# The down projection of a feed-forward layer: seven block products in place of eight, with the weight sums on VectorE and one of them made by a transfer

## The chip, the cores and the metric

The kernel runs on one core of a Trainium2 chip. The metric is device microseconds from start to end of one execution, lower is better; the time before is a median over three runs. One further execution was recorded by the hardware profiler, and every row below is from that one. The engines are TensorE (PE, its weight loads PEld), VectorE (DVE), ScalarE (ACT), GpSimd (POOL) and SyncE (SP, which here only issues transfers).

## The reference

Two layers run one after the other on 512 tokens of width 2048. The change touches only the end of the second:

```python
        x = x + y @ w_out[l]
        h = rms_norm(x, norm2_g[l])
        x = x + (jax.nn.silu(h @ ffn_w_gate[l]) * (h @ ffn_w_up[l])) @ ffn_w_down[l]
    return rms_norm(x, final_norm_g)
```

The hidden width is 5632, which the kernel cuts into 11 chunks of 512. `ffn_w_down` is 5632 x 2048, in float32.

## The kernel before

Every float32 matrix product is made of three matmuls: `split` (L135) turns a tile into a high half (`h`, an ACT cast, L136) and the rest (`l`, a DVE subtraction, L122), and the products high x high, low x high and high x low are summed in PSUM. For weights these halves are called `wh` and `wl`, for the other operand `op`. All float32 DVE additions and subtractions stand in the profile under L122, all matmuls under L112, transposes under L116.

`finish` makes the feed-forward layer in two stages. In the **gate and up stage** `fast_group` (L1632) computes, for each of the 11 chunks, both projections at once by seven products of half-size blocks in place of eight; the weight sums are formed by DVE in the raw tiles `fr` before they are split. The chunk's hidden state is transposed on PE, copied to a tile `v` by ACT (L1785) and written to the DRAM buffer `ud` (`ud<-v`).

In the **down stage** `facc` (512 tokens x 2048, float32 in SBUF) is first loaded with the residual `x3d` (L1794). `hidden(c)` (L1798) loads one chunk of `ud`, 1 MB, and splits it. `down(c)` (L1805) goes over four column blocks of 512: `block` loads the weights two 128-row blocks at a time (512 KB, `raw`), splits them (`wh`, `wl`, 128x1024), and issues 4 x 4 x 3 matmuls into four PSUM banks `psm`; DVE adds each bank to `facc` (128x512). Ten chunks make 10 x 4 x 48 = 1920 matmuls of 128x512. The **last chunk** has its weights and operand split ahead (matmuls `psm<-op,op`, 192 of them) and goes by token tile, since squares, the norm and the output transfers follow each.

No order is written out by hand: a scheduler places each engine's instructions by the program's order and by priorities (`tc.high_priority(self.ahead)` lets weight loads and splits stand far ahead of their matmuls). Each engine and each DMA queue takes its instructions strictly in that order. Pools with a fixed number of buffers decide when a tile may be written again, and memory of a closed pool is used again by the pools that open next.

## Time and the profile before

| | |
|---|---|
| median of 3 runs | 3528.2 us (3525.5 to 3532.1) |
| profiled execution | 3527.2 us |
| its span, first to last instruction | 3525.1 us |
| mean granted TensorE clock | 0.985 |
| PE busy | 3439.2 us, 98% |
| DVE busy | 2205.1 us, 63% |

Busy shares are means over the whole span, in which the gate and up stage takes some 870 us, the down stage 447 us and the last chunk with the end 58 us. Starts in the rows are us from the span's start. "Idle before" is the time for which an engine stood still ahead of an instruction, with the releaser behind it. A granted clock of 1.00 is full speed, 0.50 half of it.

### The profile page before, as it was taken

What the parts mean: (1) busy time and instruction counts of PE and PEld (TensorE: products, weight loads), DVE (VectorE), ACT (ScalarE), POOL (GpSimd) and SP (SyncE); (2) the same over time, 40 slices, a digit from 0 to 9 for tenths busy, and PEclk for the clock granted to TensorE, in tenths of its full rate; (3) what the DMA queues carried; (4) which work ended last, traced back from release to release, by engine and by line L of the source; (5) the groups of instructions that cost most, each with busy time, mean ns of one, the idle gap of its engine ahead of it and who ended that gap; (6) DMA issues with size and microseconds to landing.
All of it is one profiled execution on the core that took longest, in us unless ns stands there. A gap on an engine that the chain in (4) does not pass through costs nothing.

```text
span 3525.1 us, 48425 instructions
## 1 busy us (share of the span) xinstructions
PE 3439.2 (98%) x18730; PEld 2740.2 (78%) x18730; DVE 2205.1 (63%) x3480; ACT 1368.6 (39%) x2239; POOL 53.7 (2%) x50
## 2 busy tenths in 40 slices
PE   7999999999999999999999998999999999999998
PEld 3488887777778787788777787888888888788887
DVE  4367875566555455764566547778878778555545
ACT  3234444555433323432233334444444445322212
POOL 0000000000000000000000000000000000000000
PEclk8999999999999999999999999999999999999999
DMA  8823333222343443434434543443333334533333
GB/s 283 282 85 93 111 114 107 72 81 60 92 145 124 138 131 97 117 109 135 129 107 142 159 142 119 132 125 120 108 114 119 120 120 155 185 120 120 101 96 107
DMA packets 352601, 442.21 MB, mean 125 GB/s; under 512 B 45871, under 2 KB 200179, under 8 KB 351731
## 3 DMA queue, kind: packets, MB, share of 16 engines
q1 hardware_dynamic: 349456, 437.82, 40.7%
q8 instruction: 147, 2.41, 0.3%
q10 hardware_dynamic: 2915, 1.29, 0.1%
q14 instruction: 83, 0.68, 0.1%
HBM read 383.45 MB, written 55.57 MB: 125 GB/s over the span
## 4 chain that ended last, share of the span: by engine, by line
PE 90%; DMA 5%; DVE 3%; ACT 1%; issue 1%; SPq 0%; DVEq 0%; POOL 0%; POOLq 0%; ACTq 0%
PE acc L112 40%; PE pp L112 24%; PE psm L112 23%; DMA wm<-in_w_mod_dram 3%; PE psm L116 2%; PE pt L116 1%; DVE wl L122 1%; DMA raw<-in_ffn_w_down_dram 0%; DVE ga L132 0%; DMA ym<-ysd 0%; DMA xr<-in_x_dram 0%; DMA xr<-in_ctx_dram 0%; DVE op L122 0%; DVE u L132 0%; DMA kr<-kd 0%
## 5 line engine op out<-in xcount | busy, mean ns | idle before, releaser
L112 PE MATMUL acc<-op,wh 128*128 128x512 f32 (+2 forms) x4160 | 1243.1, 388 | 13.0 <-DVE sl L132 4.4
L112 PEld LDWEIGHTS acc<-op,wh 128*128 128x128 f32 (+1 forms) x4160 | 763.6, 189 | 198.1 <-issue 30.7
L122 DVE TENSOR_TENSOR wl<-raw,wh 128x512 fp32r<-128x512 f32 (+4 forms) x464 | 421.0, 908 | 640.3 <-ACT wh L136 589.6
L112 PE MATMUL acc<-op,wl 128*128 128x512 f32 (+2 forms) x2080 | 768.0, 389 | 4.3 <-DVE wl L122 4.1
L136 ACT CAST wh<-raw 128x512 fp32r<-128x512 f32 (+4 forms) x464 | 368.9, 796 | 996.9 <-PE acc L112 601.4
L112 PE MATMUL pp<-wh,op 128*128 128x512 f32 x2112 | 531.2, 394 | 10.3 <-ACT wh L136 10.3
L136 ACT CAST wh<-fr 128x1024 fp32r<-128x1024 f32 x308 | 323.2, 1052 | 400.9 <-PE pp L112 347.1
L112 PEld LDWEIGHTS pp<-wh,op 128*128 128x128 f32 x2112 | 397.5, 188 | 100.7 <-ACT wh L136 10.5
L112 PEld LDWEIGHTS acc<-op,wl 128*128 128x128 f32 (+1 forms) x2080 | 389.6, 189 | 97.4 <-issue 18.2
L122 DVE TENSOR_TENSOR wl<-fr,wh 128x1024 fp32r<-128x1024 f32 x308 | 371.3, 1220 | 98.1 <-ACT wh L136 63.3
L112 PE MATMUL psm<-wh,op 128*128 128x512 f32 x1280 | 396.9, 391 | 7.4 <-DVE facc L122 7.4
L112 PEld LDWEIGHTS psm<-wh,op 128*128 128x128 f32 x1280 | 241.7, 189 | 58.2 <-issue 7.8
L112 PE MATMUL pp<-wl,op 128*128 128x512 f32 x1056 | 286.0, 393 | 0.0
L112 PE MATMUL psm<-wl,op 128*128 128x512 f32 x640 | 250.6, 392 | 0.3 <-DVE wl L122 0.3
L122 DVE TENSOR_TENSOR fr<-fr,fr 128x1024 f32<-128x1024 f32 x176 | 211.2, 1221 | 50.1 <-DMA fr<-in_ffn_w_gate_dram 32.8
L112 PEld LDWEIGHTS pp<-wl,op 128*128 128x128 f32 x1056 | 197.2, 188 | 44.4 <-DVE wl L122 1.1
L122 DVE TENSOR_TENSOR facc<-facc,psm 128x512 f32<-128x512 f32 x176 | 118.0, 686 | 60.5 <-PE psm L112 54.6
L112 PEld LDWEIGHTS psm<-wl,op 128*128 128x128 f32 x640 | 120.9, 189 | 25.8 <-DVE wl L122 0.7
L112 PE MATMUL acc<-wh,op 128*128 128x256 f32 x576 | 114.8, 294 | 0.0
L112 PEld LDWEIGHTS acc<-wh,op 128*128 128x128 f32 x576 | 92.0, 193 | 5.1 <-issue 3.8
L112 PE MATMUL pp<-wh,opx 128*128 128x512 f32 x352 | 93.6, 399 | 0.0
L112 PE MATMUL acc<-wl,op 128*128 128x256 f32 x288 | 85.2, 297 | 0.3 <-DVE wl L122 0.3
(474 smaller groups left out, 3515.1 us busy)
## 6 DMA issues: line engine op xcount, KB each, us to landing
raw<-in_w_in_dram SPq DMA_DIRECT2D x216, 256.0 KB, 2.8
fr<-in_ffn_w_gate_dram SPq DMA_DIRECT2D x88, 512.0 KB, 4.8
fr<-in_ffn_w_up_dram SPq DMA_DIRECT2D x88, 512.0 KB, 4.4
raw<-in_ffn_w_down_dram SPq DMA_DIRECT2D x88, 512.0 KB, 3.8
wm<-in_w_mod_dram SPq DMA_DIRECT2D x64, 512.0 KB, 5.0
raw<-in_w_out_dram SPq DMA_DIRECT2D x64, 512.0 KB, 3.7
raw<-in_w_in_dram SPq DMA_DIRECT2D x240, 128.0 KB, 2.4
wm<-in_w_mod_dram SPq DMA_DIRECT2D x64, 256.0 KB, 2.8
```

The costliest lines, as they stand in the source:

```text
L112: self.nc.tensor.matmul(out, lhsT=l, rhs=r, start=start, stop=stop, skip_group_check=more)
L116: self.nc.tensor.transpose(out, x, self.ident[0:n, 0:n])
L122: (e or self.nc.vector).tensor_tensor(out=out, in0=x, in1=y, op=op)
L136: self.nc.scalar.copy(h, x)
```

## The change

The down stage becomes a seven-product scheme too. Two chunks are taken together (c = 0 to 4), and the columns in two halves (v = 0, 1). In each (c, v) seven products of blocks (2 x 128 tokens by 512 hidden by 512 columns, two halves u of 12 matmuls each) are made in the order 1 7 5 6 4 2 3. `onto` lets 2, 4 and 3 be summed into the PSUM banks of 1, 7 and 5. The last chunk stays as it was.

- **Operands.** The seven combinations of the hidden state are formed at the end of each gate chunk (four more DVE instructions, 128x512) and written to `ud`, 7 x 256 KB a chunk. `operands(c)` loads them from GpSimd's queue, 7 x 512 KB a pair, in rows of 1 KB, and splits them at a priority of 400.
- **Weights.** `plain` loads (SP); `total` sums on DVE for products 7, 5 and 6; for product 3 `plus` is a GpSimd transfer that adds what it reads to the tile `a11`, last used by product 6, with products 4 and 2 between.
- **Results.** Each product is added to `facc` or to `au` (sums of 1 and 6) by one DVE instruction of 128x1024; in the first pair ACT copies products 1, 7, 4, 2 and 3. Three more additions close each half of the columns.
- **Residual.** `x3d` is not loaded first: eight accumulating GpSimd transfers of 512 KB add it during the first pair.

```diff
+    def product(self, X, i, ps, h, l, j0, opens, last):
+        at = [(j0 + kk, kk, t) for kk in range(2) for t in range(2)]
+
+        for j, kk, t in at:
+            xh, xl = (x[:, j % 4, t * 128:t * 128 + 128] for x in X[j // 4][i])
+            self.mm(ps[:, t, :], xh, h[:, kk, :], opens and j == 0, False, not opens)
+            self.mm(ps[:, t, :], xl, h[:, kk, :], False, False, not opens)
...
-                v = self.t(up, [128, 2, 256], F32, "v")
+                            if c < NC - 1:
...
+                                self.tt(x5, b11, b12, ALU.subtract)
+                                self.tt(b12, b12, b22, ALU.subtract)
+                                self.stt(x6, b22, -1.0, x5, ALU.mult, ALU.subtract)
...
             with self.pool("ff1", 2) as p1, self.pool("ff2", 1) as p2:
+                wps = [self.wp2, self.wp2, p2]
                 acc = self.t(p2, [128, 4, D], F32, "facc")
-                for t in range(4):
-                    nc.sync.dma_start(out=acc[:, t, :], in_=x3d[t])
...
+                    with tc.high_priority(400):
+                        for i in order:
+                            x = raw().rearrange("p a (b t) -> p (a b) t", t=256)
+                            nc.gpsimd.dma_start(out=x, in_=ud[i - 1, 2 * c:2 * c + 2].rearrange("g f p t -> p (g f) t"))
+                            o = self.four(F32R)
...
+                    def plus(u):
+                        nc.gpsimd.dma_start(out=W["a11", u], in_=load("a12", u), accum_op=ALU.add)
+                        return W["a11", u]
+
+                    weight = {
+                        1: lambda u: plain("a11", u), 7: lambda u: total("a11", "a21", u),
+                        5: lambda u: total("a21", "a22", u), 6: lambda u: total("a11", "a22", u),
+                        4: lambda u: W["a22", u], 2: lambda u: plain("a12", u), 3: plus,
+                    }
+                    A11, A12, A21, A22, U = acc[:, 0:2, n1], acc[:, 2:4, n1], acc[:, 0:2, n2], acc[:, 2:4, n2], au[v]
+                    onto = {2: 1, 4: 7, 3: 5}
+                    to = {1: U, 7: A22, 2: A11, 5: A22, 4: A21, 6: U, 3: A12}
+                    for i in order:
+                        ps[i] = ps[onto[i]] if i in onto else bank(self.p6 if i == 6 else self.pp)
+                        for u in range(2):
+                            with tc.high_priority(self.ahead):
+                                h, l = self.halves(weight[i](u), wps)
+                            self.product(X, i, ps[i], h, l, 2 * u, i not in onto, 3)
+                        if c == 0 and i not in (5, 6):
+                            nc.scalar.copy(to[i], ps[i])
+                        else:
+                            self.tt(to[i], to[i], ps[i], ALU.subtract if i == 5 else ALU.add)
+                    if c == 0:
+                        for t in range(4):
+                            o = slice(v * 1024, v * 1024 + 1024)
+                            nc.gpsimd.dma_start(out=acc[:, t, o], in_=x3d[t][:, o], accum_op=ALU.add)
...
```

**The first place is ACT at the change of stage.** Before, the copies to `v` of the last hidden chunk are followed by casts of down weights, which wait for their loads (DMAHW), for buffers or for nothing but these:

```order
L136 CAST wh_25782<-raw_25780 128x1024 [waits DMAHW2_49,PE_49,Activation_49]
L1785 COPY v_25661<-pt_25643 128x512 [waits DMAHW5_49,PE_49,Activation_49]
L1785 COPY v_25664<-pt_25644 128x512 [waits DMAHW6_49,PE_49,Activation_49]
L136 CAST wh_25812<-raw_25810 128x1024 [waits DMAHW3_49,PE_49]
L136 CAST wh_25850<-raw_25848 128x1024 [waits DMAHW4_49,DVE_49,PE_49]
```

Now `wh_25834`, the second half of product 1, is the first tile in the memory of the new pool `ff2`, where `v` tiles lay. It waits for transfers DMAHW3 and DMAHW4, which are the second and third of the last chunk's four `ud<-v`, and all casts behind it wait with it:

```order
L1792 COPY v_25664<-pt_25646 128x512 [waits PE_49]
L1792 COPY v_25665<-pt_25647 128x512 [waits DMAHW3_49,PE_49]
L119 ACTIVATE s_25744<-p_4364_25272,h_3220_18212 128x512
L1792 COPY v_25752<-pt_25734 128x512 [waits PE_49]
L1792 COPY v_25753<-pt_25735 128x512 [waits DMAHW3_49,PE_49]
L136 CAST wh_25834<-fr_25832 128x1024 [waits DMAHW3_49,DMAHW4_49,DMAHW1_49,Activation_49]
L136 CAST wh_25874<-fr_25832 128x1024 [waits DVE_49]
L136 CAST wh_25895<-fr_25852 128x1024 [waits PE_49,Activation_49]
L136 CAST wh_25914<-fr_25871 128x1024 [waits DVE_49]
L1879 COPY au_4445_25776<-pp_25813 128x1024 [waits DMAHW2_49,PE_49]
```

**The second place is DVE in the down stage.** Before, in the middle of it, two weight remainders take turns with four additions:

```order
L122 TENSOR_TENSOR wl_27617<-raw_27614,wh_27616 128x1024 [waits DMAHW5_49,Activation_49]
L122 TENSOR_TENSOR wl_27661<-raw_27658,wh_27660 128x1024 [waits DMAHW6_49,Activation_49]
L122 TENSOR_TENSOR facc_25689<-facc_25689,psm_27580 128x512 [waits PE_49]
L122 TENSOR_TENSOR facc_25689<-facc_25689,psm_27581 128x512 [waits PE_49]
L122 TENSOR_TENSOR facc_25689<-facc_25689,psm_27582 128x512 [waits PE_49]
L122 TENSOR_TENSOR facc_25689<-facc_25689,psm_27583 128x512 [waits PE_49]
L122 TENSOR_TENSOR wl_27691<-raw_27688,wh_27690 128x1024 [waits DMAHW7_49,Activation_49]
L122 TENSOR_TENSOR wl_27729<-raw_27726,wh_27728 128x1024 [waits DMAHW0_49,Activation_49]
```

Now, from the end of half v = 0 of the second pair (product 3's `wl_26600` and `wl_26617`, which wait for the accumulating transfers, DMASW) into half v = 1, the remainders `op` of the next pair's operands stand between sums and weights. An `op` row waits for a GpSimd load (DMASW) and, by ACT, its cast:

```order
L122 TENSOR_TENSOR wl_26600<-fr_26375,wh_26599 128x1024 [waits DMASW2_49,Activation_49]
L122 TENSOR_TENSOR wl_26617<-fr_26393,wh_26616 128x1024 [waits DMASW3_49,PE_49,Activation_49]
L122 TENSOR_TENSOR facc_25775<-facc_25775,pp_26374 128x2x512 [waits PE_49]
L122 TENSOR_TENSOR wl_26637<-fr_26634,wh_26636 128x1024 [waits DMAHW4_49,Activation_49]
L122 TENSOR_TENSOR op_26894<-fr_26892,op_26894 128x1024 [waits DMASW4_49,Activation_49]
L122 TENSOR_TENSOR fr_26634<-fr_26634,fr_26672 128x1024 [waits DMAHW6_49,DVE_49]
L122 TENSOR_TENSOR wl_26655<-fr_26652,wh_26654 128x1024 [waits DMAHW5_49,PE_49,Activation_49]
L122 TENSOR_TENSOR op_26899<-fr_26897,op_26899 128x1024 [waits DMASW5_49,Activation_49]
L122 TENSOR_TENSOR fr_26672<-fr_26672,fr_26712 128x1024 [waits DMAHW0_49,DVE_49]
L122 TENSOR_TENSOR facc_25775<-facc_25775,pp_26452 128x2x512 [waits PE_49]
L122 TENSOR_TENSOR wl_26676<-fr_26634,wh_26675 128x1024 [waits Activation_49]
L122 TENSOR_TENSOR fr_26652<-fr_26652,fr_26691 128x1024 [waits DMAHW7_49,DVE_49]
```

All seven `op` rows of the next pair (here products 1, 7, 5, 6, 4, 2, 3 of the third) stand in this half v = 1, at 1, 4, 9, 14, 16, 18 and 23 rows behind the half's first row `wl_26637`; the half v = 0 ahead of it has none.

**The third place is the end of the half v = 1 on PE and the GpSimd queue.** Before, each bank was filled by plain blocks and GpSimd issued no transfer. Now product 3's first half (`wh_26858`, the tile that the transfer has added to) stands ahead of product 2's second half (bank `pp_26633`):

```order
L112 MATMUL pp_26633<-wh_26822,op_26366 128x512 [waits Activation_49]
L112 MATMUL pp_26633<-wh_26822,op_26366 128x512 x7
L112 MATMUL pp_26671<-wl_26804,op_26361 128x512 [waits DVE_49]
L112 MATMUL pp_26671<-wl_26804,op_26361 128x512 x3
L112 MATMUL pp_26711<-wh_26858,op_26371 128x512 [waits DVE_49,Activation_49]
L112 MATMUL pp_26711<-wh_26858,op_26371 128x512 x7
L112 MATMUL pp_26633<-wl_26823,op_26366 128x512 [waits DVE_49]
L112 MATMUL pp_26633<-wl_26823,op_26366 128x512 x3
```

The queue from which these come holds the next pair's seven operand loads (L1832), then the half's two accumulating transfers (L1861):

```order
L1832 DMA fr_26912<-ud_18206 128x4x256 [waits DMASW6_49,DMASW0_49,DVE_49]
L1832 DMA fr_26917<-ud_18206 128x4x256 [waits DMASW1_49,DVE_49]
L1832 DMA fr_26922<-ud_18206 128x4x256 [waits DMASW7_49,DVE_49]
L1861 DMA fr_26634<-in_ffn_w_down_dram 128x2x512 [waits DVE_49]
L1861 DMA fr_26652<-in_ffn_w_down_dram 128x2x512 [waits DVE_49]
```

## Rows read from the trace of the kernel before

**Rows 1.** The page, part 1: engines, busy us, share, instructions.

```profile
PE 3439.2 (98%) x18730; PEld 2740.2 (78%) x18730; DVE 2205.1 (63%) x3480; ACT 1368.6 (39%) x2239; POOL 53.7 (2%) x50
```

**Rows 2.** Windows: gate stage, change of stage, down stage, last chunk and end.

```profile
core 0: us, PE busy (x) PEld busy (x) DVE busy (x) ACT busy (x) POOL busy (x), PEclk, DMA share, GB/s
2150.00:3019.00 869.00, 868.98 (x3856) 709.39 (x3856) 704.69 (x640) 399.99 (x418) 0.00 (x0) 1.00 0.41 125
3019.00:3045.00 26.00, 18.58 (x77) 15.03 (x76) 8.12 (x10) 5.58 (x8) 0.00 (x0) 0.81 0.72 265
3045.00:3467.00 422.00, 421.70 (x1859) 348.59 (x1858) 211.33 (x240) 93.09 (x85) 0.00 (x0) 1.00 0.36 114
3467.00:3525.10 58.10, 45.61 (x193) 37.10 (x192) 30.56 (x49) 15.44 (x36) 2.18 (x4) 0.92 0.26 94
```

**Rows 3.** Timeline of PE: first down matmul, two waits around the down stage.

```profile
3019.65 0.39 PE L112 MATMUL psm<-wh,op 128*128 128x512 f32 x1
...
3039.06 0.77 PE L112 MATMUL psm<-wh,op 128*128 128x512 f32 x1 [7.42 <-DVE facc L122]
...
3470.78 45.40 PE L112 MATMUL psm<-op,op 128*128 128x512 f32 x192 [3.58 <-DVE facc L122]
```

**Rows 4.** Windows, same columns: inside the stages, and six us after 3039.

```profile
3060.00:3460.00 400.00, 400.00 (x1766) 331.31 (x1765) 201.99 (x229) 88.27 (x81) 0.00 (x0) 1.00 0.35 111
2245.00:2300.00 55.00, 55.00 (x241) 44.76 (x240) 40.15 (x36) 22.89 (x25) 0.00 (x0) 1.00 0.49 150
...
3039.00:3045.00 6.00, 5.94 (x14) 4.77 (x15) 1.13 (x2) 0.00 (x0) 0.00 (x0) 0.50 1.02 426
```

**Rows 5.** The chain of waits (start us, us, what) at the change of stage.

```profile
3019.82 7.06 PE psm L112 x31
...
3027.61 0.59 ACT v L1785
...
3028.22 4.93 DMA ud<-v
...
3033.21 4.83 DMA facc<-x3d
...
3039.06 12.70 PE psm L112 x42
```

**Rows 6.** Groups by line, 2150 to 3019 us: busy us, mean ns | idle.

```profile
L122 DVE TENSOR_TENSOR wl<-fr,wh 128x1024 fp32r<-128x1024 f32 x308 | 371.3, 1220 | 98.1 <-ACT wh L136 63.3 <-PE pp L112 33.8
L136 ACT CAST wh<-fr 128x1024 fp32r<-128x1024 f32 x306 | 321.2, 1052 | 400.9 <-PE pp L112 347.1 <-DVE fr L122 26.0 <-issue 11.1
...
L132 DVE SCALAR_TENSOR_TENSOR s<-s,un 128x512 f32<-128x512 f32 x22 | 14.2, 685 | 0.0
...
L122 DVE TENSOR_TENSOR un<-pp,un 128x1024 f32<-128x1024 f32 x11 | 13.5, 1224 | 14.0 <-PE pp L112 14.0
```

**Rows 7.** Timeline of DVE inside a gate chunk.

```profile
2874.74 1.22 DVE L122 TENSOR_TENSOR fr<-fr,fr 128x1024 f32<-128x1024 f32 x1
2875.88 1.22 DVE L122 TENSOR_TENSOR wl<-fr,wh 128x1024 fp32r<-128x1024 f32 x1
```

**Rows 8.** DMA issues, 2150 to 3019 us: count, KB, median us to landing.

```profile
fr<-in_ffn_w_gate_dram SPq DMA_DIRECT2D x84, 512.0 KB, 4.8
...
ud<-v SPq DMA_DIRECT2D x40, 256.0 KB, 2.2
op<-ud SPq DMA_DIRECT2D x6, 1024.0 KB, 5.8
raw<-in_ffn_w_down_dram SPq DMA_DIRECT2D x5, 512.0 KB, 6.4
```

**Rows 9.** The same of the down stage, 3045 to 3467 us.

```profile
raw<-in_ffn_w_down_dram SPq DMA_DIRECT2D x79, 512.0 KB, 3.8
```

**Rows 10.** The loads of x3d: issues, who waited, time to landing.

```profile
L1794 SPq DMA_DIRECT2D facc<-x3d x4: 332/430/647, 3033.2 to 3034.5; - x4
...
DMA to landing us min/median/max: 9.9/9.9/9.9
```

More of the change, by code (lines that the diff above doesn't have):

```diff
@@ L1628, in halves @@
         return h, l
+    def product(self, X, i, ps, h, l, j0, opens, last):
[4 more added lines that the diff above has]
+            self.mm(ps[:, t, :], xl, h[:, kk, :], False, False, not opens)
+        for j, kk, t in at:
+            xh = X[j // 4][i][0][:, j % 4, t * 128:t * 128 + 128]
+            self.mm(ps[:, t, :], xh, l[:, kk, :], False, j == last, not opens)
     def fast_group(self, srcs, X, rp, cp, wps, parts):
@@ L1657, in part @@
                 h, l = self.halves(weight[i](u), wps)
-            at = [(2 * u + kk, kk, t) for kk in range(2) for t in range(2)]
-            for j, kk, t in at:
-                xh, xl = (x[:, j % 4, t * 128:t * 128 + 128] for x in X[j // 4][i])
-                self.mm(ps[i][:, t, :], xh, h[:, kk, :], opens and j == 0, False, not opens)
-                self.mm(ps[i][:, t, :], xl, h[:, kk, :], False, False, not opens)
-            for j, kk, t in at:
-                xh = X[j // 4][i][0][:, j % 4, t * 128:t * 128 + 128]
-                self.mm(ps[i][:, t, :], xh, l[:, kk, :], False, j == 7, not opens)
+            self.product(X, i, ps[i], h, l, 2 * u, opens, 7)
         def bank():
@@ L1722, in finish @@
                 made = [0]
+                fx = iter(range(100))
                 def tiles():
@@ L1782, in finish @@
                                     self.tr(pt[f // 2][:, o:o + 128], s[:, f * 128:f * 128 + 128])
+                            vs = [self.t(uv, [128, 2, 256], F32, "v") for _ in range(2)]
                             for k in range(2):
[L1784 to L1787 removed]
@@ L1805, in down @@
-                def down(c, hs):
-                    for b in range(4):
-                        ps = [self.psm() for _ in range(4)]
-                        self.block(wd[c * 512:c * 512 + 512], [(b * 512, 512)], 4,
-                                   [(ps[t], "t", (t, 0), hs, True, True) for t in range(4)])
-                        for t in range(4):
-                            v = acc[:, t, b * 512:b * 512 + 512]
-                            self.tt(v, v, ps[t], ALU.add)
-                hs = [hidden(0), hidden(1)]
@@ L1815, in finish @@
-                for c in range(NC - 1):
-                    down(c, hs[c])
-                    if c + 2 < NC:
-                        hs.append(hidden(c + 2))
-                c = NC - 1
-                W = []
-                for b in range(4):
-                    h4, l4 = self.four(F32R), self.four(F32R)
-                    for k in range(0, 4, 2):
-                        raw = self.t(self.wp, [128, 2, 512], F32, "raw")
-                        nc.sync.dma_start(out=raw, in_=wd[c * 512 + k * 128:c * 512 + k * 128 + 256, b * 512:b * 512 + 512].rearrange("(k p) c -> p k c", p=128))
-                        self.split(h4[:, k:k + 2, :], l4[:, k:k + 2, :], raw)
-                    W.append((h4, l4))
+                au = [self.t(p2, [128, 2, 512], F32, f"au{v}") for v in range(2)]
@@ new lines, in raw, with bank, operands @@
+                def raw():
+                    return self.t(rp, [128, 2, 512], F32, "fr")
+                def bank(pool):
+                    return self.t(pool, [128, 2, 512], F32, "pp")
+                order = (1, 7, 5, 6, 4, 2, 3)
+                def operands(c):
+                    X = {}
+                    with tc.high_priority(400):
[3 more added lines that the diff above has]
+                            o = self.four(F32R)
+                            h, l = (o[:, k:k + 2, :].rearrange("p a (b t) -> p (a b) t", t=256) for k in (0, 2))
+                            self.split(h, l, x)
+                            X[i] = (h, l)
+                    return [X]
@@ new lines, in finish @@
+                X = operands(0)
+                for c in range(NC // 2):
+                    down(c, 0, X)
+                    down(c, 1, X)
+                    if c + 1 < NC // 2:
+                        X = operands(c + 1)
+                c = NC - 1
+                with tc.high_priority(400):
+                    u = self.four(F32)
+                    for i, f, o in ((1, 0, 0), (5, 0, 256), (2, 2, 0), (3, 2, 256)):
+                        nc.sync.dma_start(out=u[:, f:f + 2, o:o + 256], in_=ud[i - 1, c].rearrange("f p t -> p f t"))
+                    uh, ul = self.four(F32R), self.four(F32R)
+                    self.split(uh, ul, u)
+                    W = []
+                    for b in range(4):
+                        h4, l4 = self.four(F32R), self.four(F32R)
+                        for k in range(0, 4, 2):
+                            r = raw()
+                            nc.sync.dma_start(out=r, in_=wd[c * 512 + k * 128:c * 512 + k * 128 + 256, b * 512:b * 512 + 512].rearrange("(k p) c -> p k c", p=128))
+                            self.split(h4[:, k:k + 2, :], l4[:, k:k + 2, :], r)
+                        W.append((h4, l4))
+                    fg = []
+                    for i in range(2):
+                        fg.append(raw())
+                        nc.sync.dma_start(out=fg[i].rearrange("p a b -> p (a b)"),
+                                          in_=a["final_norm_g_2"][i * 1024:i * 1024 + 1024].rearrange("(o d) -> o d", o=1).to_broadcast([128, 1024]))
```

88 lines of the change are left out of this document (57 added, 31 removed).

## The prediction

> **What bounds the kernel now.** I read the page's shares first, then busy time by stage, then the timeline of PE at the stages' edges. PE is busy for 98% of the span, DVE for 63%, ACT for 39%, POOL for 2% with 50 instructions [rows 1]. A mean over the whole span says little of one stage, so the windows come next: in the gate stage PE is busy for 868.98 of 869.00 us, in the down stage for 421.70 of 422.00, in both at a granted clock of 1.00; DVE is busy for 704.69 us (81%) of the first and for 211.33 us (50%) of the second [rows 2]. So the down stage is bound by the number of its matmuls, and DVE has half of its time free there. What is not matmul stands at the edges. PE waits 7.42 us for the first addition to `facc`, ahead of the matmul at 3039.06, and 3.58 us ahead of the last chunk [rows 3]. The chain says what the first wait is made of: the last copies to `v`, 4.93 us until `ud<-v` has landed, 4.83 us for `facc<-x3d` [rows 5]. Behind that wait the clock stands at 0.50 for some 6 us, in which 14 matmuls are done [rows 4].
>
> One matmul takes 400/1766 = 0.2265 us in the down stage and 55/241 = 0.2282 us in the gate stage, where the seven-product form already runs [rows 4].
>
> **What the change removes.** Five pairs x 2 halves x 7 products x 24 are 1680 matmuls in place of 1920: 240 fewer, x 0.2265 = 54.4 us. The wait for `x3d` goes, since nothing is loaded into `facc` first: 7.4 us, and with it the half clock, in which 14 matmuls took 6.0 us and not 3.2: 2.8 us. The wait of 3.6 us ahead of the last chunk is taken out here and its heir put in below. The new matmuls run at the gate stage's pace: 1680 x 0.0017 = 2.9 us back. Sum: 54.4 + 10.2 + 3.6 - 2.9 = **65.3 us**.
>
> **What it adds.** *Gate stage.* Four DVE instructions of 128x512 a chunk, nearest row 685 ns [rows 6]: 2.7 us in a chunk of some 79 us, 81% to 84% for DVE, and three more writes of 256 KB. PE never waited there, so the cover is DVE's free 19%; between 0 and 3 us, I take 1.
>
> *Change of stage (first place of the order).* The cast of product 1's second half now waits for the third `ud<-v`. The last copies to `v` come at 3027.6 and the writes are issued at 3028.2 [rows 5]; landing takes between 2.2 us, the median [rows 8], and 4.93 us [rows 5], and the cast 1.05 us [rows 6], so these weights are there between 3031.5 and 3034.2. Until then PE has two halves (24 matmuls, 5.4 us behind 3019.65) and the transposes, to about 3026.9. It stands still for 4.6 to 7.3 us, and the clock may fall as it did behind the wait of 7.42 us, 2 to 2.8 us more. Below that: nothing, if the writes land sooner. I take 8. So most of the 10.2 us gained here is given back at the same place.
>
> *DVE in the down stage (second place).* In a half, PE has 168 matmuls, 168 x 0.2282 = 38.3 us. DVE has 14 weight remainders, 6 sums and 7 additions of products, 27 instructions of 1024 columns, and the seven operand remainders all in v = 1: 34. One takes 1.22 us by itself [rows 6], but back to back they start 1.14 us apart [rows 7]. So v = 0 costs DVE 30.8 us and v = 1 38.8 us: over both, 69.6 of 76.6 us, 91%, and in v = 1 nothing is free. What holds DVE up there, comes through to PE.
>
> The candidate is the operand loads, of 512 KB with rows of 1 KB, from GpSimd, L us each. Before has no transfer from GpSimd. The nearest are 512 KB from SP at 3.8 [rows 9], 4.8 and 6.4 us [rows 8], the 1 MB `op<-ud` at 5.8 us [rows 8] and 9.9 us for the 1 MB of `facc<-x3d`, four at once [rows 10]. Product 1's operand uses the buffer that `wl_26600` frees, three rows ahead of its own remainder: 3 x 1.14 less the cast of 1.05 hides 2.4 us. Operand 5 uses operand 1's buffer (seven rows between, 6.9 us hidden), operand 4 uses operand 5's (six, 5.8 us). DVE falls behind by (L - 2.4), (L - 6.9) and (L - 5.8), where positive, less some 2 us that it is ahead. At L = 3.8 nothing reaches PE; at 6.4 it is 2.6 us a pair, at 8 some 7, at 10 some 13. I take 6.4, the 512 KB load in busy queues, and 3 us for the three pairs that load another under full DVE load: 9. In the first pair ACT takes five of seven additions, but four `x3d` transfers stand among the operand loads on GpSimd's queue: 0 to 6, I take 3. In the last, the weights of the last chunk (eight remainders) take the operands' place: 0 to 4, I take 2.5.
>
> *The accumulating transfer (third place).* From product 6's remainder, the last reader of `a11`, to product 3's first matmul PE has 64 matmuls in v = 0 (14.6 us) and 48 in v = 1 (11.0 us), counted in its order. Less the cast, a transfer of A us is hidden to 13.5 and 10 us. The bounds are 3.8 [rows 9] and 9.9 us [rows 10], so its cost is nothing, by the narrowest cover of 10 us; beyond it, each us costs one for each of five halves, and beyond 13.5 us for each of ten.
>
> The Trainium skill, page "DMA: Bandwidth & Descriptors", section "Anatomy of one DMA — SWDGE (gpsimd) path", gives a transfer from GpSimd 2.0 us and its bytes over 436 GB/s, an estimate of 3.2 us for 512 KB. By that the pairs' 9 us would go and the time be 3477. No row of before shows such a transfer.
>
> **The sum.** 65.3 - 1 - 8 - 3 - 9 - 2.5 = 41.8 us. The profiled execution took 3527.2 us (2.1 us outside its span), 1.0 us under the median; 3528.2 - 41.8 is **3486 us**.
>
> **Rivals.** *(a) Hardly a stall.* In the gate stage DVE at 81% held PE up for nothing at all [rows 2], and loads of 3.8 us exist. Then only the change of stage costs, 5 to 8, and 2 to 4 elsewhere: 3470 to 3476. Against it: 91% is not 81%.
>
> *(b) DVE becomes the bound.* Operand loads at L = 8 to 10: 21 to 39 us in the three pairs, 15 to 21 at the edges and in the first and last pair, so 3500 to 3523. For it: ACT and DVE work strictly in order, and one late load holds up all sums behind it.
>
> *(c) The accumulating transfer is late; slower.* It reads, adds and writes, and shares one queue with seven operand loads and, at first, eight of `x3d`. If A is 20 us, five halves wait 10 us and five 6.5: 82 us, less the 56 left of the 65.3 when only the edges are paid: 3554. It decides from A = 17.4 us on, where 10A - 117.5 reaches 56. Against it: 9.9 us is the longest landing of four 1 MB loads at once [rows 10]. What would do it is a transfer that can't start while DVE works, with DVE at 91% and no row of before that shows both.
>
> The Trainium skill has a rule of this kind ("SBUF — State Buffer", section "Who interferes with whom"): a VectorE instruction with two inputs in SBUF keeps a GpSimd instruction that reads SBUF out until it ends, and a transfer from GpSimd can be starved of its descriptors. It counts the starving to VectorE's two-port modes and infers that a two-input addition leaves the descriptors alone, so I give it 0.02 of this rival's 0.08; its time would be that of (c). No row of before shows it.
>
> *(d) Nothing comes of it*: the stalls of (b) and a little of (c) eat the 65 us, within 0.2% of before (7 us, about what a measurement of this kernel can tell from no change).
>
> **How the numbers follow.** My forecast (3479 to 3495) has 0.40, (a) 0.27, (b) 0.19, (c) 0.08, (d) 0.06. The range leaves out (c), (d), the far end of (b) and the lowest of (a): 3458 to 3512. Faster by over 0.2% is the forecast, (a) and (b), 0.86; within it (d) with 0.05; slower (c) and the rest of (d), 0.09.
>
> **What would show it.** Right: 1680 matmuls in the down stage some 0.228 us apart; one wait of 5 to 7 us of PE near 3027, ended by ACT's cast, with `ud<-v` behind it; DVE busy for about 90% of the stage; PE's other waits short, in halves v = 1, released by DVE or ACT rows that wait for operand loads; accumulating transfers landing in under 10 us. Wrong: PE waiting ahead of product 3 (then A is long), waits of over 5 us in each pair (L), waits in v = 0 as well (DVE's instructions are slower than 1.14 us beside the transfers), or a gate stage longer than before by several us.

## The result, and the profile after

The changed kernel took **3491.9 us** (median of 4 runs, 3485.3 to 3494.0) beside 3526.8 us for the kernel before: ratio 0.9898, 95% interval 0.9885 to 0.9911. It is 35 us faster, where 42 were forecast. The profiled execution took 3492.6 us, with a span of 3490.8 us and a mean granted clock of 0.985.

The page, part 1, answers to [rows 1]: 240 matmuls fewer, and 146 us more of DVE.

```profile
PE 3394.7 (97%) x18490; PEld 2697.5 (77%) x18490; DVE 2351.2 (67%) x3571; ACT 1454.5 (42%) x2334; POOL 112.1 (3%) x113
```

The windows of the stages answer to [rows 2]. They are cut at the first matmul of the gate stage, at the first one behind that stage's last, and at the first of the last chunk; two matmuls of the down stage (0.5 us) stand at 3022.21, ahead of the second cut:

```profile
core 0: us, PE busy (x) PEld busy (x) DVE busy (x) ACT busy (x) POOL busy (x), PEclk, DMA share, GB/s
2152.48:3023.60 871.12, 871.12 (x3859) 711.39 (x3860) 726.47 (x686) 396.90 (x420) 6.49 (x8) 1.00 0.42 135
3023.60:3436.99 413.39, 395.73 (x1692) 319.38 (x1690) 350.34 (x305) 192.57 (x192) 52.56 (x56) 0.98 0.63 179
3436.99:3490.80 53.81, 44.65 (x197) 36.61 (x195) 24.95 (x43) 11.41 (x32) 2.20 (x4) 0.93 0.21 78
```

PE is still busy for every microsecond of the gate stage, though DVE is busier there. The down stage takes 413.4 us from the second cut to the last chunk's first matmul; before it took 3470.78 - 3019.65 = 451.1 us [rows 3]. That is -37.7 us. The end is 0.5 us shorter (54.3 before, by [rows 3] and the span). The rest of the span's 34.3 us lies ahead of the down stage, which begins at 3023.60 and not at 3019.65: +4.0 us. The gate stage as such was not longer (871.1 us; from its first matmul at 2147.83 it took 871.8 before), so this comes from the part ahead of it. The change leaves that part as it was, and the gate stage's first matmul comes anywhere from 2147.4 to 2158.7 us in the traces of the kernels of this document. So the 4.0 us lie within the scatter between executions.

The timeline of PE at the waits, where [rows 3] had 7.42 and 3.58 us:

```profile
3035.89 3.78 PE L112 MATMUL pp<-wh,op 128*128 128x512 f32 x8 [3.73 <-ACT wh L136]
...
3345.41 6.29 PE L112 MATMUL pp<-wh,op 128*128 128x512 f32 x16 [3.73 <-ACT wh L136]
...
3410.47 2.54 PE L112 MATMUL pp<-wh,op 128*128 128x512 f32 x8 [2.69 <-ACT wh L136]
```

The first is the wait at the change of stage. The second lies 10 us ahead of the last pair of chunks: by 3345.40 PE had done 1307 matmuls that write `pp` (the first of them still the gate stage's), and with the two at 3022.21 some 1308 of the 4 x 336 = 1344 of four pairs. So it is near the end of the fourth pair, ahead of the second half of product 2. Only the third lies in the last pair, in its half v = 1. The count for `pp` alone (without a column for POOL):

```profile
3023.60:3345.40 321.80, 305.17 (x1307) 245.55 (x1305) 53.43 (x44) 10.08 (x10) 0.99 0.68 192
```

Behind each of the three waits the granted clock fell towards half (1.2 in place of 2.4 GHz). Windows of these places, columns as above:

```profile
3034.00:3040.00 6.00, 4.11 (x10) 3.24 (x11) 4.06 (x4) 2.33 (x3) 0.00 (x0) 0.51 0.16 56
...
3345.40:3351.70 6.30, 6.29 (x17) 5.01 (x18) 6.30 (x5) 2.91 (x3) 0.00 (x0) 0.59 0.60 204
3410.40:3418.40 8.00, 7.93 (x28) 6.39 (x29) 6.31 (x6) 6.01 (x7) 2.40 (x2) 0.79 0.39 115
```

At 0.2265 us each [rows 4] these 10, 17 and 28 matmuls would have taken 2.3, 3.9 and 6.3 us in place of 4.1, 6.3 and 7.9: the half clock cost 1.8, 2.4 and 1.6 us.

All waits of PE from 3015 to 3470 us, as the line waited for, us in total, times, longest:

```profile
PE pp L112 <- ACT wh L136: 15.5, 9, 3.7
PE pt L116 <- DVE s L132: 1.2, 2, 0.7
PE pp L112 <- DVE wl L122: 1.0, 2, 0.7
```

Of these 17.7 us the three waits shown are 10.2, so all that PE waited elsewhere in the down stage is 6.3 us (and 1.2 us for the transposes). The timeline of ACT says what was behind the three:

```profile
3034.79 1.04 ACT L136 CAST wh<-fr 128x1024 fp32r<-128x1024 f32 x1 [1.74 <-DMA ud<-v]
...
3342.52 1.90 ACT L136 CAST op<-op 128x2048 fp32r<-128x2048 f32 x1 [8.93 <-DMA op<-ud]
...
3409.37 2.16 ACT L136 CAST wh<-fr 128x1024 fp32r<-128x1024 f32 x2 [6.31 <-DVE fr L122]
```

The first is the cast that the order pointed at, waiting for the write of the last hidden chunk. The second is the split of the last chunk's hidden state, whose loads stand early in SP's queue (issued from 3329.8 to 3332.2) and landed some 10 us later; three weight casts stand behind it on ACT and come late. The third is another matter: the cast waited for a sum on DVE, and DVE had no time left there:

```profile
3391.00:3411.00 20.00, 17.31 (x75) 13.82 (x74) 19.53 (x18) 9.68 (x10) 0.00 (x0) 1.00 0.44 147
```

Among its 18 instructions are four remainders of the last chunk's weights (`op<-fr,op`).

DMA issues of the down stage (KB each, median us to landing):

```profile
fr<-in_ffn_w_down_dram SPq DMA_DIRECT2D x78, 512.0 KB, 4.8
fr<-ud POOLq DMA_DIRECT2D x28, 512.0 KB, 4.3
fr<-in_ffn_w_down_dram POOLq DMA_DIRECT2D x20, 512.0 KB, 7.6
facc<-x3d POOLq DMA_DIRECT2D x8, 512.0 KB, 8.2
```

The operand loads take 4.3 us, where 6.4 was taken in the prediction. The accumulating transfers take 7.6 us at the median and at most 11.0.

### The profile page after: what moved, and what is told of

Same layout as the page of the kernel before. It is cut to its first block, busy times and chain, and to the rows that moved or that the text cites. A ratio compares the mean times of both kernels' runs of the same rounds, so it can differ in the third digit from the quotient of the medians.

```text
span 3490.8 us, 48449 instructions
## 1 busy us (share of the span) xinstructions
PE 3394.7 (97%) x18490; PEld 2697.5 (77%) x18490; DVE 2351.2 (67%) x3571; ACT 1454.5 (42%) x2334; POOL 112.1 (3%) x113
## 5 line engine op out<-in xcount | busy, mean ns | idle before, releaser
L112 PE MATMUL pp<-wh,op 128*128 128x512 f32 x3232 | 814.9, 395 | 25.8 <-ACT wh L136 25.8
L112 PEld LDWEIGHTS pp<-wh,op 128*128 128x128 f32 x3232 | 610.2, 189 | 167.7 <-ACT wh L136 29.7
L136 ACT CAST wh<-fr 128x1024 fp32r<-128x1024 f32 x448 | 468.3, 1052 | 559.4 <-PE pp L112 444.0
L122 DVE TENSOR_TENSOR wl<-raw,wh 128x512 fp32r<-128x512 f32 (+4 forms) x384 | 323.1, 842 | 468.7 <-ACT wh L136 425.8
L122 DVE TENSOR_TENSOR wl<-fr,wh 128x1024 fp32r<-128x1024 f32 x448 | 541.0, 1219 | 124.1 <-ACT wh L136 81.1
L136 ACT CAST wh<-raw 128x512 fp32r<-128x512 f32 (+4 forms) x384 | 284.8, 742 | 689.7 <-PE acc L112 611.5
L112 PE MATMUL pp<-wl,op 128*128 128x512 f32 x1616 | 435.5, 393 | 1.0 <-DVE wl L122 1.0
L112 PEld LDWEIGHTS pp<-wl,op 128*128 128x128 f32 x1616 | 303.4, 188 | 69.1 <-DVE wl L122 2.2
L122 DVE TENSOR_TENSOR fr<-fr,fr 128x1024 f32<-128x1024 f32 x236 | 283.4, 1219 | 36.1 <-DMA fr<-in_ffn_w_gate_dram 21.7
L112 PEld LDWEIGHTS pp<-wh,opx 128*128 128x128 f32 x352 | 65.4, 188 | 14.1
```

The source lines that it names most:

```text
L112: self.nc.tensor.matmul(out, lhsT=l, rhs=r, start=start, stop=stop, skip_group_check=more)
L122: (e or self.nc.vector).tensor_tensor(out=out, in0=x, in1=y, op=op)
L136: self.nc.scalar.copy(h, x)
```

## The experiments

**1. The third weight set gets memory of its own.** The wait at the change of stage is there because the third pair of weight halves stands in a pool that opens where `v` lay. Here the gate stage's third set (pool `fw`) stays open through the down stage, on the other side of SBUF.

```diff
-                with self.pool("fc", 1) as cp, self.pool("fu", 2) as up, self.pool("fv", 4) as uv, self.pool("fw", 1) as fw:
+                fw_pool = self.pool("fw", 1, side="right")
+                fw = fw_pool.__enter__()
+                with self.pool("fc", 1) as cp, self.pool("fu", 2) as up, self.pool("fv", 4) as uv:
...
-                wps = [self.wp2, self.wp2, p2]
+                wps = [self.wp2, self.wp2, fw]
```

> Against the changed kernel (3491.9 us): the third set of weight halves keeps its own memory from the gate stage into the down stage, so no cast waits for the writes of the last hidden chunk. Edge theory: the 3.73 us wait of PE at the change of stage and most of the half clock behind it (9 matmuls in 4.0 us, for 2.05) go, 4 to 7 us, so 3485 to 3488 us. Rival, the copies into facc and au, which lie in memory of the same age, take the wait over: under 2 us.

Measured: 3477.2 us (3474.0 to 3481.2), ratio 0.9857, 95% 0.9837 to 0.9878. The wait is gone, as expected. But the gain over the changed kernel is 14.7 us, more than the 4 to 7 us expected, and a new wait stands in the first pair. The timelines of POOL, ACT and PE there:

```profile
3051.46 1.82 POOL L1887 DMA_DIRECT2D facc<-x3d  x2 [3.85 <-ACT facc L1881]
3052.61 1.46 POOL L1834 DMA_DIRECT2D fr<-ud  x1
...
3061.40 1.04 ACT L136 CAST op<-fr 128x1024 fp32r<-128x1024 f32 x1 [6.48 <-DMA fr<-ud]
...
3063.44 6.33 PE L112 MATMUL pp<-wh,op 128*128 128x512 f32 x16 [3.70 <-ACT wh L136]
```

An operand load issued behind two accumulating transfers of `x3d` landed 8.8 us later, and the weight cast behind its cast was late. This is the prediction's first-pair mechanism; in the changed kernel, where PE comes to this place later, all waits of the first pair but that at the change of stage are 0.9 us. So PE waited nearly as long in all, 16.4 us against 17.7. In the trace the gate stage, where nothing waits in either kernel, is 9.1 us shorter (862.0 us), and the down stage 6.8 (406.6 us). The gain must be for the most part in the matmuls themselves, to which experiments 5 and 6 go.

**2. Product 3's sum by DVE.** No accumulating weight transfers; four 1.2 us additions a pair more on DVE.

```diff
-                        4: lambda u: W["a22", u], 2: lambda u: plain("a12", u), 3: plus,
+                        4: lambda u: W["a22", u], 2: lambda u: plain("a12", u), 3: lambda u: total("a11", "a12", u),
```

> The third sum is made by DVE from the tile that product 2 has loaded, and the 20 accumulating weight transfers are gone. DVE theory: 29 and 36 instructions of 1.14 us in the two halves, 33 and 41 us against 38.3 us of PE, so the halves v = 1 of the pairs 1 to 3 gain some 3 us of waits each and the last pair more: 10 to 20 us over the changed kernel, 3502 to 3512 us. Rival, the transfers themselves are what holds the stage up (7.6 us each, on the DMA engines): as fast or up to 5 us faster.

Measured: 3491.4 us (3489.0 to 3496.5), 0.9899, 0.9878 to 0.9920: no difference from the changed kernel. The window of pairs two and three, from the changed kernel's trace:

```profile
3106.00:3270.00 164.00, 159.96 (x694) 129.65 (x693) 142.52 (x124) 74.76 (x74) 23.77 (x26) 1.00 0.69 197
```

and from this one's:

```profile
3106.00:3270.00 164.00, 160.51 (x696) 130.12 (x695) 149.57 (x131) 76.33 (x74) 14.13 (x18) 1.00 0.57 170
```

DVE went from 87% to 91%, and PE has as little idle time as before. So DVE's load was not what made PE wait in these pairs, and moving the sum into a transfer bought nothing. The edit also takes away 20 transfers (DMA share 0.57 for 0.69), so a small loss by DVE and a small gain by the queues may cancel here; the run does not part them.

**3. No products between.** Product 3 stands right behind 6, with the transfer between them.

```diff
-                order = (1, 7, 5, 6, 4, 2, 3)
+                order = (1, 7, 5, 6, 3, 4, 2)
```

> Order 1 7 5 6 3 4 2: product 3 follows product 6 at once, so the accumulating transfer has no two products to hide behind. Cover theory: PE has some 16 matmuls (3.7 us) between the last reader of the tile and product 3, against 7.6 us of landing and 1.05 us of cast: 5 us of wait in each of ten halves and up to 2 us of half clock behind it, 50 to 70 us over the changed kernel, 3540 to 3560 us. Rival, transfers from GpSimd are slack at any place, because casts and sums in their order set the pace: 0 to 15 us.

Measured: 3538.5 us (3530.2 to 3542.9), 1.0028, 1.0016 to 1.0039, slower than the kernel before and 46.6 us over the changed one, a little under the 50 to 70 expected. The waits of PE, then of ACT, from 3015 to 3480 us:

```profile
PE pp L112 <- ACT wh L136: 46.1, 20, 6.0
...
ACT wh L136 <- DMA fr<-in_ffn_w_down_dram: 86.3, 19, 9.2
```

In the changed kernel that ACT row is 7.6 us in 3 times. The landing time is the same (7.7 us median against 7.6): the two products do not make the transfer faster, they hide it. They are worth more than the whole change.

**4. The residual alone.** The kernel before, with `facc` not loaded first: ACT copies the first chunk's banks, and four accumulating transfers of 1 MB add `x3d` behind it.

```diff
-                for t in range(4):
-                    nc.sync.dma_start(out=acc[:, t, :], in_=x3d[t])
...
+                            if c == 0:
+                                nc.scalar.copy(v, ps[t])
+                            else:
+                                self.tt(v, v, ps[t], ALU.add)
...
+                    if c == 0:
+                        for t in range(4):
+                            nc.gpsimd.dma_start(out=acc[:, t, :], in_=x3d[t], accum_op=ALU.add)
```

> The kernel before with one part of the change alone: the residual isn't loaded into facc ahead of the first additions; ACT copies the first chunk's products and four accumulating transfers add x3d after it. Edge theory: PE then waits only for the landing of the last ud writes, whose memory facc reuses (to about 3034 and not 3039 us), 4 to 8 us less than before: 3519 to 3523 us. Rival, the wait at this edge is another's (weights, casts): no change, 3527 us.

Measured: 3540.4 us (3536.6 to 3545.8), 1.0037, 1.0026 to 1.0048: slower, against the expectation. PE's timeline at the edge and in the next chunk:

```profile
3033.91 0.50 PE L112 MATMUL psm<-wh,op 128*128 128x512 f32 x1 [2.21 <-ACT facc L1811]
...
3083.41 0.79 PE L112 MATMUL psm<-wh,op 128*128 128x512 f32 x1 [3.97 <-DVE facc L122]
3095.67 1.22 PE L112 MATMUL psm<-wh,op 128*128 128x512 f32 x2 [9.34 <-ACT wh L136]
```

and its chain of waits between them:

```profile
3066.88 25.82 DMA op<-ud
```

The edge did give back what was expected (2.21 for 7.42 us). But a plain 1 MB load on SP's queue, issued 1.1 us behind the four transfers, took 25.8 us; in the kernel before its kind takes 5.8 us [rows 8]. So in this form the edge's gain was lost again where the accumulating transfers met a load that PE needed soon. The changed kernel has them in eight pieces of 512 KB, two at a time; that this is what spares it was not tested by itself.

**5. Starts of tiles modulo 64 bytes.** In the trace of experiment 1 more matmuls fit into the same time than in the changed kernel. What its edit also moved is the third set's address. A first theory was that a matmul is slower where its two operands' starts differ modulo 64 bytes. An unused tile of 32 bytes in the first pool moves all behind it; this was done to the changed kernel (pad_all), to the kernel before (before_pad) and to experiment 1's (keep_pad).

```diff
             q3 = self.t(f0, [128, 4], F32, "q3")
+            self.t(f0, [128, 8], F32, "pad")
```

> The changed kernel with one tile of 32 bytes a partition, never written or read, ahead of the feed-forward layer's tiles, so that opx and the third set of weight halves start 32 bytes past a multiple of 64, as op and the other weight halves do. Address theory (a matmul takes 0.2335 and not 0.2265 us where its two operands differ in their start modulo 64 bytes, in the trace every third set of 12): 1408 matmuls of the gate stage and 560 of the down stage x 0.007, 14 us less than the changed kernel, 3478 us, with the wait of 3.73 us at the change of stage still there. Rival, it is the low memory region or the separate pool that is slow: no change, 3492 us.

> The kernel before with the same 32 bytes. Address theory: 1408 matmuls of its gate stage x 0.007, 10 us less than before, 3517 us; its down stage, with two sets of weight halves, does not change. Rival: no change.

> The third set's own memory from the earlier run, and the 32 bytes. Address theory: there the weights agree with op already and only the 528 matmuls with opx are left slow, x 0.007: 4 us less than the earlier 3477, 3473 to 3474 us, and nothing at the change of stage. Rival: no change, 3477 us.

Measured: 3489.2 us (0.9888, 0.9874 to 0.9903), 3527.9 us (0.9998, 0.9988 to 1.0007), 3481.1 us (0.9863, 0.9846 to 0.9881): each the same as without the tile. The theory fell.

**6. Starts modulo 256 bytes.** In the compiled programs the operand tiles `op` and two of the three weight sets start at 224 modulo 256, and in the gate stage before and after `opx` and the third set at 0. A tile of 224 bytes in place of 32 brings these to 224 as well (pad_224, on the changed kernel). The kernel before with `fw` on the other side, where its start is 224, is the same test without the change (before_keep).

```diff
+            self.t(f0, [128, 56], F32, "pad")
```

```diff
-                with self.pool("fr", 10, side="right") as rp, self.pool("fc", 1) as cp, self.pool("fu", 2) as up, self.pool("fw", 1) as fw:
+                with self.pool("fr", 10, side="right") as rp, self.pool("fw", 1, side="right") as fw, self.pool("fc", 1) as cp, self.pool("fu", 2) as up:
```

> The changed kernel with 224 bytes in place of the 32 of the earlier run, so that in the gate stage opx and the third set of weight halves agree with op and the other sets in their start modulo 256 bytes, in the down stage the third set modulo 128 alone. Theory of a larger unit (128 or 256 bytes): the third set's 12 matmuls take 0.2265 us each like the others in the gate stage, and in the down stage as well if the unit is 128; 10 to 14 us less than the changed kernel, 3478 to 3482 us. Rival, the address has no part in it, and the slow pace belongs to tiles of the pools that open and close inside the layer on the low side of the memory: the pace as before, 3489 to 3492 us.

> The kernel before with its third set of weight halves moved in the same way to the other side of the memory, next to the raw tiles, for the gate stage. If the pace of the third set is a matter of its place, 3168/3 of the gate stage's matmuls with op lose 0.007 us each, and those with opx and this set gain it: 6 to 10 us less than before, 3517 to 3521 us. Rival, what made the earlier run quick is bound to the down stage's form: no change, 3527 us.

Measured: pad_224 3476.7 us (3472.6 to 3480.5), 0.9856, 0.9842 to 0.9869, 15 us below the changed kernel; before_keep 3517.2 us (3510.4 to 3520.7), 0.9973, 0.9963 to 0.9983, 8 us below the kernel before. The timeline of PE in a gate chunk of the changed kernel:

```profile
2305.22 2.02 PE L112 MATMUL pp<-wh,opx 128*128 128x512 f32 x8
...
2308.01 0.85 PE L112 MATMUL pp<-wh,opx 128*128 128x512 f32 x3
...
2314.40 1.98 PE L112 MATMUL pp<-wh,op 128*128 128x512 f32 x8
...
2317.12 1.10 PE L112 MATMUL pp<-wh,op 128*128 128x512 f32 x4
```

The starts are to be compared: 12 matmuls with `opx` from 2305.22 to 2308.01 take 2.79 us, 12 with `op` from 2314.40 to 2317.12 take 2.72. The same timeline of pad_224, in the gate stage and then in the down stage:

```profile
2287.45 1.98 PE L112 MATMUL pp<-wh,opx 128*128 128x512 f32 x8
...
2290.17 1.98 PE L112 MATMUL pp<-wh,opx 128*128 128x512 f32 x8
...
3205.25 2.02 PE L112 MATMUL pp<-wh,op 128*128 128x512 f32 x8
...
3208.04 1.99 PE L112 MATMUL pp<-wh,op 128*128 128x512 f32 x8
```

Twelve with `opx` now take 2.72 us too. So it is 0.2325 us a matmul in the one kind of group and 0.2267 in the other. In the down stage of pad_224 the third set starts at 96, and its groups stay slow (2.79 us from 3205.25 to 3208.04): agreement modulo 128 is not enough. Agreement modulo 256 parts the quick groups from the slow ones in the kernels before, after and of experiments 1 and 6. It is not the whole of it. In pad_all both `opx` and the third set start at 32, and yet their twelve, from 2372.86 to 2375.62, take 2.76 us, about halfway between 2.72 and the 2.80 of the twelve ahead of them, which start at 224 and 32:

```profile
2370.06 2.03 PE L112 MATMUL pp<-wh,opx 128*128 128x512 f32 x8
...
2372.86 2.01 PE L112 MATMUL pp<-wh,opx 128*128 128x512 f32 x8
...
2375.62 1.99 PE L112 MATMUL pp<-wh,op 128*128 128x512 f32 x8
```

The quick pace of 2.72 us is shown where both start at 224; why the chip does this is open. The two stages of pad_224 say where its 15 us lie:

```profile
2147.99:3006.84 858.85, 858.81 (x3859) 711.26 (x3860) 723.44 (x684) 396.57 (x419) 6.50 (x8) 1.00 0.43 136
3006.84:3420.23 413.39, 393.15 (x1691) 317.44 (x1690) 351.08 (x307) 192.98 (x192) 52.56 (x56) 0.99 0.64 181
```

The gate stage is 12.3 us shorter than in the changed kernel and the down stage, whose third set stays slow, as long as there. In before_keep the gate stage takes 862.3 us for 871.8.

**7. The last chunk's hidden state comes later.** On experiment 5's keep_pad: the load of the last chunk's hidden state moves from SP's queue, early, to GpSimd's in the middle of the last pair, and its split with it. The copy of a few numbers from `facc` only ties its place to the end of v = 0.

```diff
+                    if c == NC // 2 - 1:
+                        u = self.four(F32)
+                        nc.vector.tensor_copy(u[:, :, ::256], acc[:, :, 0:512:256])
+                        for i, f, o in ((1, 0, 0), (5, 0, 256), (2, 2, 0), (3, 2, 256)):
+                            nc.gpsimd.dma_start(out=u[:, f:f + 2, o:o + 256], in_=ud[i - 1, NC - 1].rearrange("f p t -> p f t"))
+                        uh, ul = self.four(F32R), self.four(F32R)
+                        self.split(uh, ul, u)
...
-                    u = self.four(F32)
-                    for i, f, o in ((1, 0, 0), (5, 0, 256), (2, 2, 0), (3, 2, 256)):
-                        nc.sync.dma_start(out=u[:, f:f + 2, o:o + 256], in_=ud[i - 1, c].rearrange("f p t -> p f t"))
-                    uh, ul = self.four(F32R), self.four(F32R)
-                    self.split(uh, ul, u)
```

> As the run with both, and the last chunk's hidden state is loaded and split in the middle of the last pair, behind the half v = 0, and not ahead of it. Theory of the end: ACT's wait of some 9 us for this load, with weight casts behind it, is what makes the wait of 4 us at the start of the last pair and the half clock behind it, so 4 to 6 us less; but its remainder (128x2048, 2.3 us of DVE) now stands in the last half, where DVE has the last chunk's weights as well, so up to 3 us come back there: 1 to 6 us less than keep_pad. Rival, DVE alone sets the last pair's pace: the wait moves, no change or up to 3 us more.

Measured: 3468.8 us (3466.6 to 3469.8), 0.9828, 0.9814 to 0.9843, 12 us below keep_pad and 8 below experiment 1. From the first matmul behind the gate stage to the end the two traces differ by 5.7 us (462.2 and 456.4); the rest of the 12 lies ahead, where the edit changes nothing. By these traces the edit is worth some 6 us, the upper end of what was expected. The two waits of over 1 us at the end of the fourth pair and in the last, in keep_pad:

```profile
3333.51 6.42 PE L112 MATMUL pp<-wh,op 128*128 128x512 f32 x16 [3.70 <-ACT wh L136]
3398.97 2.67 PE L112 MATMUL pp<-wh,op 128*128 128x512 f32 x8 [3.74 <-ACT wh L136]
```

and all waits here, from 3330 to 3430 us:

```profile
3404.86 2.11 PE L112 MATMUL pp<-wh,op 128*128 128x512 f32 x8 [0.73 <-ACT wh L136]
3407.72 3.02 PE L112 MATMUL pp<-op,op 128*128 128x512 f32 x12 [0.76 <-DVE facc L122]
...
3412.26 1.20 PE L112 MATMUL pp<-wl,op 128*128 128x512 f32 x4 [0.61 <-DVE wl L122]
...
3417.40 4.83 PE L112 MATMUL pp<-op,op 128*128 128x512 f32 x20 [1.21 <-DVE facc L122]
```

Both waits are gone, and with them the half clock; 3.3 us of small ones are left. The first was made by the place of this load and split, not by a shortage of DVE's time: DVE's work is the same. The edit puts the load on another queue too, so place and queue are not told apart. The second was DVE's, as the changed kernel's trace shows. Here the eight remainders of the last chunk's weights come behind this split, from 3400.78 on, some 28 us into the half v = 1 and not from its start. So they were moved as well, and it is with this order, and no less work, that the second wait went.

**8. All together.** Experiment 7's kernel with the 224-byte tile.

> The third set in its own memory, the last chunk's hidden state in the middle of the last pair, and the 224 bytes for opx. Theory of the larger unit: the 528 matmuls with opx lose 0.007 us each, 4 us less than the 3469 of the run without: 3465 us. Rival: no change from 3469 us.

Measured: 3465.2 us (3457.4 to 3467.4), 0.9817, 0.9803 to 0.9832. This is the fastest version that does all the work, 26.7 us below the changed kernel. Its interval overlaps that of experiment 7; what the tile adds shows in the traces, where the gate stage is 4.6 us shorter (858.6 for 863.2). Its largest wait is the first pair's, 3.32 us, behind the `x3d` transfers.

**9. What bounds it then.** On experiment 8's kernel; this one leaves out 240 of the down stage's matmuls.

```diff
-            self.mm(ps[:, t, :], xl, h[:, kk, :], False, False, not opens)
+            if last == 7 or i not in (1, 7, 5):
+                self.mm(ps[:, t, :], xl, h[:, kk, :], False, False, not opens)
```

> The version of best (third set's pool kept open, 224 B tile, last chunk's hidden state loaded early) with the low x high matmuls of products 1, 7 and 5 left out in the down stage: 240 of its 1800 or so matmuls are not done, so the output is incomplete; VectorE's, ScalarE's and the DMAs' work stays. If TensorE alone sets the pace of the down stage, it falls by 240 x 0.2265 = 54 us below best, to about 3411 us. If VectorE, busy some 69.6 us for each pair of chunks beside 65.2 us that TensorE would then need, takes over as the bound, the gain stops near 30 us, at about 3435 us, and VectorE's busy share in the windows of the pairs goes above 95%.

Measured: 3452.3 us (3446.5 to 3458.4), 0.9775, 0.9755 to 0.9795, 13 us below experiment 8 by the medians, 15 by the ratios. Both theories missed. A window inside the pairs, experiment 8's:

```profile
3106.00:3350.00 244.00, 238.60 (x1039) 195.49 (x1038) 214.83 (x187) 110.05 (x107) 32.67 (x35) 0.99 0.61 177
```

and with fewer matmuls:

```profile
3106.00:3350.00 244.00, 221.07 (x923) 175.25 (x923) 224.00 (x196) 113.78 (x112) 32.78 (x35) 0.97 0.66 186
```

with the waits of PE, then of DVE, in the same stretch:

```profile
PE pp L112 <- DVE wl L122: 12.9, 7, 3.9
PE pp L112 <- ACT wh L136: 9.9, 10, 2.3
...
DVE wl L122 <- ACT wh L136: 5.5, 5, 2.4
DVE wl L122 <- issue: 5.0, 4, 1.9
```

PE falls from 98% to 91%, DVE rises from 88% to 92%. By the matmuls recorded in the windows a pair takes 244 x 336/1039 = 78.9 us in the first and 244 x 288/923 = 76.1 us in the second. DVE's 69.6 us a pair, by the prediction's count, are 75.7 us at 92%. So TensorE is the bound of experiment 8, but with less than 3 us a pair in hand. The nearest reading of what follows, not shown by a run, is that DVE, in its strict order, becomes the bound at 92% and not at 100%, since it waits in between for ACT's casts; how much of that is late weight loads was not taken apart.

## Why the prediction was right, point by point

**Removed.** 240 x 0.2265 = 54.4, the edge's 10.2 and the 3.6 us are what left the trace. With what PE waits now (17.7) and the half clock (1.8 + 2.4 + 1.6 = 5.8) the down stage would be 44.7 us shorter; it is 37.7 us shorter, 37.2 with the two matmuls ahead of the cut. The 7.5 us between them are for the most part a slower pace of 1680 matmuls, where the prediction had 2.9. It read 0.2282 us from the gate stage as the pace of the seven-product form. By experiment 6 that figure was a mixture: 0.2267 in some groups, 0.2325 in others. The third set of the down stage starts at 128, the operand at 224. Its group at 3051.61 in the changed kernel's trace is followed by the others at 3054.42, 3057.16 and 3059.88: 2.81, 2.74 and 2.72 us. So the group behind a slow one is a little slow too, and three groups take 0.11 us more than 3 x 2.72. In 1680 matmuls there are 46.7 such threes: 5.1 us. Eight transposes of the last hidden chunk, which stood ahead of the stage before, make some 0.7 us more (four take 0.35 at 3025.88). What made up the rest was not isolated.

**Gate stage.** Taken 1 us; measured none (871.1 us, PE busy throughout).

**Change of stage.** Taken 8 us; measured 0.5 + 0.67 + 3.73 us of waits (the first two are of the transposes) and 1.8 of half clock: 6.7. Experiment 1, where this wait is gone, shows that the cause was the one named.

**First pair and pairs 1 to 3.** Taken 3 + 9; measured 6.3 us of short waits and, at the end of the fourth pair, 3.73 with 2.4 of half clock: 12.4. The sum is right, and half of it by luck. The short waits are of the kind forecast: all stand in halves v = 1, ended by ACT's or DVE's weight rows, and ACT waited for operand loads there 38.4 us in 22 times. But they cost half of what was taken, since L came out at 4.3 us (4.1 to 11.6), not at 6.4. By the prediction's own formula a load of 4.3 us costs nothing; that the longest loads made what is left was not shown. The Trainium skill, page "DMA: Bandwidth & Descriptors", section "Anatomy of one DMA — SWDGE (gpsimd) path", gives an estimate of 3.2 us for 512 KB; the measured 4.3 decides, and is nearer to that than what was taken.

**The step that was left out.** The other 6.1 us are a term that the prediction put at nothing: the load of the last chunk's hidden state, whose cast stands on ACT ahead of weight casts of the fourth pair. The prediction looked at DVE's instructions there and not at this load. Experiment 7 shows that moving it takes the wait away.

**Last pair.** Taken 2.5, in a range of 0 to 4; measured 2.69 of wait and 1.6 of half clock, 4.3. The mechanism was the one named, the remainders of the last chunk's weights on a DVE that is busy for 19.53 of 20 us; the half clock behind it was not in the sum.

**Accumulating transfer.** Taken nothing. A is 7.6 us, at most 11.0, inside the cover of 10 and 13.5 us for nearly all: ACT waited 7.6 us in three times for them. Experiment 3 shows the cover's worth.

**The sum.** Forecast: 68.2 removed, 2.9 for the pace, 23.5 added, 41.8 us. Measured in the down stage: 68.2 removed, 7.5 for the pace and the transposes, 17.7 + 5.8 = 23.5 added, 37.2 us. What was added comes to the forecast's figure only because errors cancel: operand loads that cost half of what was taken, and a load that was not seen. Cut at 3023.60, the stage gives 37.7 us; with 0.5 us more at the end, and 4.0 us lost ahead of it, within the scatter, the span is 34.3 us shorter.

**The rivals.** *(a)* had the operand loads right (6.3 us is little) and failed by the load at the end of the fourth pair, the last pair and the pace; experiment 8, without these and without the wait at the change of stage, comes to 3465 us, below its 3470 to 3476. *(b)* took DVE for the next thing to give way; experiment 2 put more on DVE at no cost in the pairs two and three. DVE did give way in the last pair, for 4.3 us, and by experiment 9's windows it would be the bound some 3 us a pair further down. *(c)* needed A of 17.4 us. Such times do exist: experiment 4's four transfers of 1 MB at once landed after 11.2 to 25.2 us. The Trainium skill, page "SBUF — State Buffer", section "Who interferes with whom", infers that a VectorE addition with two inputs leaves the descriptors of a transfer from GpSimd alone. The trace agrees: with DVE busy for 85% of the down stage (350.34 of 413.39 us) the longest landing of an accumulating transfer of weights was 11.0 us.

## What to carry to other kernels

A cheap transfer in place of an engine's work is worth what stands between its issue and its reader: count that cover in the reader's engine's time before counting the transfer's. When a stage is taken over by a new scheme, look for the waits where it meets its neighbours, above all which tile's memory the first new tile takes and where the next stage's first load stands in its queue; here these two cost 6.7 and 6.1 us beside a gain of 54. And a pace that is 1 to 3% off between two places of one kernel is worth asking for a cause: here the start of tiles was worth 12 to 15 us beside the 35 of the change. And where two runs differ, ask first in which stage: 4 to 5 us of some differences here lay ahead of everything that was changed.

## What was not expected of the hardware

- Matmuls of 128x512 took 0.2325 us in some groups and 0.2267 in others, 2.6% apart. In most groups it goes by whether the two operands' starts in SBUF agree modulo 256 bytes; with both at 32 (pad_all) it was 0.230. Moving the tiles was worth 15 us in the changed kernel (12.3 of them in the gate stage of its trace) and 8 us in the kernel before (9.5).
- Accumulating transfers of weights from GpSimd, of 512 KB, took 7.6 us beside 4.3 us for plain ones of operands of the same size and queue. Beside four of 1 MB a load on another queue took 25.8 us for some 5.8.
- With the clock at half behind waits of 2.7 to 3.7 us, each such wait cost 1.6 to 2.4 us more than itself.
